# Four places for the tiles of h, and a quarter of a weight pair loaded ahead

## The chip, the cores and the metric

The kernel runs on one core of a Trainium2 chip. The metric is the device time of one execution in microseconds (us), as the median of several runs. Engines are named as in the profile: PE (TensorE, the matmuls; PEld is its weight load), DVE (VectorE), ACT (ScalarE), POOL (GpSimd) and SP (SyncE, whose queue issues almost all DMAs of this kernel). Each engine takes its own instructions in order.

## The reference

One decoder layer on x of 1024 tokens by 1024 features, in float32:

```
xn  = rmsnorm(x, attn_norm_g)
proj = xn @ w_in                      # q, k, v of two head groups, forget logits
out_a = sliding-window attention with sinks and ALiBi      # 8 heads, 2 kv heads
out_b = forgetting attention (causal, decay by cumsum of log f)   # 8 heads
h   = x + concat(out_a, out_b) @ w_out
hn  = rmsnorm(h, mlp_norm_g)
y   = h + square(relu(hn @ w_up)) @ w_down                 # w_up 1024 x 4096
```

## The kernel before

Activations are kept transposed: features on the 128 partitions, the 1024 tokens along the free axis, in two halves `left` and `right` of 512. Each float32 operand of a matmul is split into a high and a low part, and each product is three matmuls (high x high, high x low, low x high). A split is one cast, mostly on ACT, that makes the high part, and one subtraction on DVE or POOL that makes the low part (line 77 and line 80 of the helper `split`).

The order of the work is: the input projection and attention; beside the end of attention, the first half of the out projection (`out_first`: mix slices 0 to 3 of every output slice, plus x, stored to `part_d` in HBM); then the second half; then the up products; then the down products. The function that writes the kernel lists instructions in program order; a planner with a timeline of its own, under priorities, sets the order in which each engine gets them, so that an instruction can go ahead of others that precede it in the text. `tc.issue_after(ins)` keeps what is written under it behind `ins` on the same engine.

The change lies at the seam between the out projection and the up products. An output slice `dt` (0 to 7) is 128 features of h by 1024 tokens. For each, `out_products` runs 24 matmuls (mix slices 4 to 7), and `out_finish(dt, ps)` then does the following:

- it loads the first half's sum from `part_d` into a tile `h` (line 986), adds the matmul result to it on DVE (line 988, one add per token half) and stores h to `h_d` (line 989), since the end of the kernel needs h again;
- it makes the operands of the up products from it. These products use a scheme of Strassen's kind (seven products in place of eight for a 2 x 2 block), so their operands `bh[n]`, `bl[n]` are splits of h's blocks and of sums `ts` of blocks. Slices 0 to 3 and 4 to 7 are the two feature blocks. For `dt < 4` there is one split (operand 1) and one sum; for `dt >= 4` two splits (operands 2 and 3), three sums and four splits of sums (operands 6, 7, 5, 4).

Slices come in the order 0, 4, 1, 5, 2, 6, 3, 7. The products of 0 and 4 are partly done beside attention; the others follow in the loop `for dt in (1, 5, 2, 6, 3, 7)`. The tiles of h take turns in two places: slices 0 to 3 in the slot `w2`, slices 4 to 6 in `w3`; slice 7 has a place of its own, `rr`. A slot that is used again waits for the readers of its former tile, the store to `h_d` among them.

Slots are named places in SBUF (`slot(tag, ...)`), used by one tile after another. Those that matter here: `m1`, `m2`, `m3`, `r1` held mix slices 0 to 3 (read in the first half), `r0` and `m4` hold mix slices 4 and 5 (read in the second half). `r1` holds the sums `ts`. `tmp` is a small tile of 2 KB a partition, used later by the squares of h.

The up weights come in 16 pairs `j`. `up_load(j)` loads a pair with two DMAs of 512 KB into `raws[j]`; a raw pair has four quarters, `a11, a12, a21, a22`. `up_sum(j)` makes the weight sums on DVE, `up_weights(n, src)` splits one operand's weights, and `up(j)` runs the seven products in the order `UP = (1, 2, 3, 6, 7, 5, 4)`, 12 matmuls each. Pairs 0 and 1 are loaded ahead: pair 0 into `m3` behind the last mix load, pair 1 into `m2` behind the load of h's slice 5. While slices 3 and 7 are finished, the weights of product 1 for `j = 0` and for `j = 1` (quarter `a11` of pair 1) are already split; PE runs both products 1 first, back to back, and then products 2, 3, 6, 7, 5, 4 of `j = 0`. From `j = 1` on the results `hb` of the up products lie in `m2`.

Of the kernel before, what the change touches and what calls it, by code (L numbers as in the profile page):

```python
# [8 lines left out]
F32 = mybir.dt.float32  # L9
# [7 lines left out]
P = 128  # L17
D = 1024
S = 1024
KT = D // P  # L20
# [5 lines left out]
NJ = NF // 2  # L26
# [29 lines left out]
def hybrid_layer(  # L56
# [13 lines left out]
    nc = tc.nc  # L70
# [4 lines left out]
    def split(hi, lo, src, hi_eng, lo_eng):  # L75
        if hi_eng is nc.scalar:
            hi_eng.copy(hi, src)  # L77
        else:
            hi_eng.tensor_copy(hi, src)
        return lo_eng.tensor_tensor(out=lo, in0=src, in1=hi.bitcast(F32), op=ALU.subtract)  # L80
# [32 lines left out]
    def small_vectors():  # L113
# [26 lines left out]
    o = {"zl": ctx.enter_context(  # L140
        tc.tile_pool(name="zl", bufs=1, side="left", reuse_waits="tile")
    )}

    def slot(tag, name, shape, dt=F32, pool=None):
        pool = o[pool or ("zx" if tag == "w6" else "zw" if tag[0] == "w" else "zl")]
        return pool.tile([P] + shape, dt, tag=tag, name=name, bufs=1)
# [722 lines left out]
    def out_weights(dt, e0):  # L869
        i = nout[0] = nout[0] + 1  # L870
        wr = o["zw"].tile([P, 4, P], F32, tag="wor", name="wor", bufs=2)
        nc.sync.dma_start(wr, w_o[dt][:, e0 : e0 + 4, :])
        w = slot(WOS[i - 10] if i > 9 else f"w{i % 2}", "wos", [2, 4, P], F32R)
        split(w[:, 0], w[:, 1], wr, nc.scalar, nc.gpsimd)
        return w[:, 0], w[:, 1]
# [12 lines left out]
    def out_products(ps, w, es):  # L888
        wh, wl = w
        for e in es:  # L890
            j = e % 4
            for c in range(2):
                cs = slice(c * 512, (c + 1) * 512)
                mm(ps[c], wh[:, j, :], mh[e][:, cs], j == 0, False)
                mm(ps[c], wh[:, j, :], ml[e][:, cs], False, False)
            for c in range(2):
                cs = slice(c * 512, (c + 1) * 512)
                mm(ps[c], wl[:, j, :], mh[e][:, cs], False, j == 3)
# [72 lines left out]
    rr = o["zr"].tile([P, S], F32, name="rr")  # L971
    left, right = slice(0, 512), slice(512, 1024)
    part = {}

    def h_split(n, t, src, gain):
        hi, lo = bh[n][:, t, :], bl[n][:, t, :]
        part["cast"] = nc.scalar.activation(hi, src, AF.Copy, scale=gain)  # L977
        nc.vector.scalar_tensor_tensor(  # L978
            out=lo, in0=src, scalar=gain, in1=hi.bitcast(F32), op0=ALU.mult, op1=ALU.subtract
        )  # L980

    def out_finish(dt, ps):
        t, gain = dt % 4, gm[:, dt : dt + 1]
        h = slot(f"w{2 + dt // 4}", "h", [S]) if dt < 7 else rr
        with tc.issue_after(part["load"].ins) if dt == 7 else nullcontext():
            part["load"] = nc.sync.dma_start(h, part_d[dt])
        for c, cs in enumerate((left, right)):
            nc.vector.tensor_tensor(out=h[:, cs], in0=ps[c], in1=h[:, cs], op=ALU.add)
        nc.sync.dma_start(h_d[dt], h)
        if dt < 4:  # L990
            h_split(1, t, h[:, left], gain)
            ts = part["t"] = slot("r1", "ts", [4, 512])
            b12 = part["b12"] = slot("w4", "b12", [512])
            part["cast"] = nc.scalar.activation(b12, h[:, right], AF.Copy, scale=gain)
            nc.vector.scalar_tensor_tensor(
                out=ts[:, 0], in0=h[:, left], scalar=gain, in1=b12, op0=ALU.mult, op1=ALU.subtract
            )
            return
        ts, b12 = part["t"], part["b12"]
        h_split(2, t, h[:, left], gain)  # L1000
        h_split(3, t, h[:, right], gain)
        for i, q, other, op in (
            (1, right, ts[:, 0], ALU.add),
            (2, right, b12, ALU.subtract),
            (3, left, ts[:, 1], ALU.subtract),
        ):
            nc.vector.scalar_tensor_tensor(
                out=ts[:, i], in0=h[:, q], scalar=gain, in1=other, op0=ALU.mult, op1=op
            )
        part["rest"] = lambda: sum_splits(ts, t, ((0, 5), (3, 4)))  # L1010
        sum_splits(ts, t, ((1, 6), (2, 7)))
        if t < 3:
            part.pop("rest")()

    def sum_splits(ts, t, which):
        for i, n in which:
            split(bh[n][:, t], bl[n][:, t], ts[:, i], nc.scalar, nc.vector)

    raws, up_loads, up_sums = {}, {}, {}

    def up_load(j):
        raws[j] = slot({0: "m3", 1: "m2"}.get(j, f"r{j % 2}"), "wur", [2, KT, P])
        for i in range(2):
            up_loads[j] = nc.sync.dma_start(raws[j][:, i], w_u[j + i * NJ])

# [3 lines left out]
    def plus(out, a, b, eng=nc.vector):  # L1029
        eng.tensor_tensor(out=out, in0=a, in1=b, op=ALU.add)  # L1030

    def up_sum(j):
        raw = raws.pop(j)
        s = slot("m5" if j % 2 == 0 else "m4" if j > 1 else "r1", "wus", [4, 4, P])
        a11, a12, a21, a22 = raw[:, 0, :4], raw[:, 0, 4:], raw[:, 1, :4], raw[:, 1, 4:]
        plus(s[:, 0], a21, a22)
        minus(s[:, 1], s[:, 0], a11)
        minus(s[:, 2], a11, a21)
        minus(s[:, 3], a12, s[:, 1])
        return {1: a11, 2: a12, 3: s[:, 3], 4: a22, 5: s[:, 0], 6: s[:, 1], 7: s[:, 2]}  # L1040
# [3 lines left out]
    def w_slot(name, shape, dt=F32):  # L1044
        nw[0] += 1
        return slot(f"w{(1, 5, 0, 6, 3, 4, 2)[(nw[0] - 1) % NW]}", name, shape, dt)

    def up_weights(n, src):
        w = w_slot("wu", [2, 4, P], F32R)
        split(w[:, 0], w[:, 1], src, nc.scalar, nc.vector if n in (2, 6, 5) else nc.gpsimd)  # L1050
        return w
# [3 lines left out]
    for dt, ps, w in ahead_of:  # L1055
        out_finish(dt, ps)
# [7 lines left out]
    def bank(name):  # L1064
        nbank[0] += 1
        return pm.tile([P, 512], F32, tag=f"m{nbank[0] % 8}", name=name, bufs=1)

    casts = []
    for dt in (1, 5, 2, 6, 3, 7):
        w = out_weights(dt, 4)  # L1070
        ps = [bank(f"po{c}") for c in range(2)]
        out_products(ps, w, range(4, 8))
        out_finish(dt, ps)
        if dt == 5:
            with tc.issue_after(part["load"].ins):
                up_load(1)
        casts.append(part["cast"].ins)
        if dt == 3:
            up_ahead = [up_weights(1, up_sums[0][1]), up_weights(1, raws[1][:, 0, :4])]

# [3 lines left out]
    def up_products(n, w, ps):  # L1086
        for k in range(4):
            mm(ps, w[:, 0, k], bh[n][:, k], k == 0, False)
            mm(ps, w[:, 0, k], bl[n][:, k], False, False)
            mm(ps, w[:, 1, k], bh[n][:, k], False, k == 3)  # L1090
# [1 line left out]
    second = []  # L1092

    def up(j):
        if 0 < j < NJ - 1:
            up_load(j + 1)
        src = up_sums.pop(0) if j == 0 else up_sum(j)
        m = {}
        for n in UP:
            if n == 1 and j == 1:  # L1100
                m[n] = second.pop()
            else:
                with tc.issue_after(casts[-2 if n == 2 else -1]) if j == 0 else nullcontext():
                    w = up_ahead.pop(0) if n == 1 and j == 0 else up_weights(n, src[n])
                m[n] = bank(f"pu{n}")
                up_products(n, w, m[n])
            if n == 1 and j == 0:
                second.append(bank("pu1"))
                up_products(1, up_ahead.pop(), second[0])
            if n == 2 and j == 0:  # L1110
                part.pop("rest")()
            if n == 2 and j == 1:
                nbank[0] += 1
            if n == 1:
                u = slot("m1", "u", [4, 512])
                b = slot("m2" if j else "m0", "hb", [4, 512])
                nc.scalar.copy(u[:, 0], m[1])
            if n == 2:
                plus(b[:, 0], m[2], u[:, 0])
            if n == 6:  # L1120
                plus(u[:, 1], m[6], u[:, 0])
            if n == 7:
                plus(u[:, 2], m[7], u[:, 1])
            if n == 5:
                minus(u[:, 3], u[:, 1], m[5])
                minus(b[:, 2], u[:, 2], m[5])
                plus(b[:, 3], m[3], u[:, 3])
            if n == 4:
                plus(b[:, 1], m[4], u[:, 2])
        return lambda: up_end(j, b)  # L1130
# [14 lines left out]
    tmp = lambda name, n: o["zr"].tile([P, n], F32, tag="tmp", name=name, bufs=1)  # L1145
# [192 lines left out]
    for i in range(len(STEPS)):  # L1338
        down(i)
        if STEPS[i][0] == len(PHASES) - 1 and late:  # L1340
            name, dt, cs = late.pop(0)
# [65 lines left out]
```

## Time and profile before

| | us |
|---|---|
| median of 3 runs | 1085.82 |
| lowest and highest of the runs | 1085.18, 1089.3 |
| the profiled execution | 1086.83 |
| its span, first to last instruction | 1085.1 |

The span has 15578 instructions, and the mean granted TensorE clock over it is 0.998 of full speed. The stages by the trace: attention and the first half of the out projection up to 427 us, the second half up to 465 us, the up products up to 776 us, the down products to the end.

How to read it: a line of the timeline gives the start, the duration, the engine, the line of the kernel, the operation, the tile written and the tiles read, how many instructions the line merges, and in brackets how long the engine had been idle and what ended that. In a table by stretches, each row gives the stretch and its length, then busy time and instruction count of PE, PEld, DVE, ACT and (where it is not left out for want of instructions) POOL, then the granted PE clock, the busy share of the DMA engines and GB/s. A line of waits gives the total, the number of times and the longest. A line of the chain that ended last gives start, length and what held the chain. A line of DMA issues gives the count, the size of one and the median time from issue to landing.

### The profile page before, as it was taken

To read this page: it belongs to the slowest core of one execution; us is meant where nothing else is said; L and a number is where in the kernel's file an instruction comes from. 1 tells how busy PE (TensorE), PEld (TensorE's weight loads), DVE (VectorE), ACT (ScalarE), POOL (GpSimd) and SP (SyncE) were. 2 spreads that over 40 slices of the span, in tenths; PEclk is the share of its full clock that TensorE was granted. 3 is DMA by queue.
4 is the path that set the end of the run, shared out by engine and by line. 5 is a ranking of instruction groups with operands and counts; after the bars stand their busy time and mean duration, and the time that the engine had idled before them with its cause. 6 is when DMAs were issued, how large, how long until landed. Compare 5 with 4: busy or idle time off the path is not lost.

```text
span 1085.1 us, 15578 instructions
## 1 busy us (share of the span) xinstructions
PE 1072.6 (99%) x5492; PEld 932.6 (86%) x5492; DVE 780.5 (72%) x1319; ACT 574.3 (53%) x1022; POOL 384.2 (35%) x350
## 2 busy tenths in 40 slices
PE   9999999999999999999999999999999999999998
PEld 8999999999998887878888888888888888888886
DVE  7377787877775787897776869674775876764395
ACT  5558587776867765555445453534533433333331
POOL 5572423546556663213223332322222313131100
PEclk9999999999999999999999999999999999999999
DMA  8402212324746655644455443443998885665523
GB/s 289 162 14 61 61 44 65 117 90 138 245 164 251 232 191 181 228 160 171 168 186 184 175 172 136 151 158 131 354 390 311 307 296 205 229 233 190 172 85 116
DMA packets 96222, 195.67 MB, mean 180 GB/s; under 512 B 7392, under 2 KB 19856, under 8 KB 96144
## 3 DMA queue, kind: packets, MB, share of 16 engines
q1 hardware_dynamic: 95856, 194.54, 51.3%
q8 instruction: 43, 0.70, 0.3%
q14 instruction: 35, 0.29, 0.1%
q10 hardware_dynamic: 288, 0.15, 0.0%
HBM read 141.61 MB, written 53.04 MB: 179 GB/s over the span
## 4 chain that ended last, share of the span: by engine, by line
PE 90%; DVE 4%; DMA 2%; issue 1%; ACT 1%; POOL 1%; SPq 0%; ACTq 0%; DVEq 0%
PE pu L73 28%; PE pd L73 28%; PE ps L73 13%; PE po L73 7%; PE pvb L73 3%; PE spb L73 3%; PE tpb L740 3%; PE sp L73 1%; PE tpa L565 1%; PE pv L73 1%; DMA xq<-in_x_dram 1%; DMA wr<-in_w_a_dram 1%; PE ptk L331 1%; PE ptq L331 1%; DVE x L207 1%
## 5 line engine op out<-in xcount | busy, mean ns | idle before, releaser
L73 PE MATMUL pd<-hx,wx 128*128 128x512 f32 (+1 forms) x1350 | 304.9, 388 | 0.0
L73 PEld LDWEIGHTS pd<-hx,wx 128*128 128x128 f32 x1350 | 252.7, 188 | 52.2
L73 PE MATMUL pu<-bh,wu 128*128 128x512 f32 x896 | 278.0, 391 | 1.2 <-ACT bh L977 1.2
L73 PEld LDWEIGHTS pu<-bh,wu 128*128 128x128 f32 x896 | 168.9, 189 | 37.2 <-ACT bh L977 1.6
L73 PE MATMUL ps<-w,x 128*128 128x384 f32 (+1 forms) x960 | 196.5, 342 | 0.9 <-POOL w L80 0.6
L73 PE MATMUL pu<-bl,wu 128*128 128x512 f32 x448 | 175.1, 391 | 0.6 <-DVE bl L978 0.6
L73 PEld LDWEIGHTS ps<-w,x 128*128 128x128 f32 x960 | 165.1, 188 | 5.0 <-POOL w L80 1.2
L77 ACT CAST hx<-hr 128x1024 fp32r<-128x1024 f32 x56 | 59.0, 1054 | 175.5 <-PE pd L73 171.0
L80 POOL TENSOR_TENSOR wx<-wda,wx 128x1024 fp32r<-128x1024 f32 x24 | 65.3, 2720 | 195.6 <-ACT wx L77 177.3
L80 DVE TENSOR_TENSOR hx<-hr,hx 128x1024 fp32r<-128x1024 f32 x56 | 72.3, 1300 | 71.0 <-ACT hx L77 71.0
L73 PEld LDWEIGHTS pu<-bl,wu 128*128 128x128 f32 x448 | 84.5, 189 | 18.6 <-DVE bl L978 0.9
L73 PE MATMUL po<-mix,wos 128*128 128x512 f32 x384 | 93.6, 393 | 0.0
L80 POOL TENSOR_TENSOR wu<-wus,wu 128x512 fp32r<-128x512 f32 x32 | 46.4, 1451 | 129.0 <-ACT wu L77 129.0
L73 PEld LDWEIGHTS po<-mix,wos 128*128 128x128 f32 x384 | 70.7, 188 | 13.8
L80 POOL TENSOR_TENSOR wu<-wur,wu 128x512 fp32r<-128x512 f32 x32 | 43.0, 1344 | 91.5 <-ACT wu L77 91.5
L77 ACT CAST wu<-wus 128x512 fp32r<-128x512 f32 x64 | 38.4, 618 | 62.6 <-PE pu L73 56.2
L1027 DVE TENSOR_TENSOR ht<-hb 128x512 f32<-128x512 f32 x32 | 22.9, 756 | 63.2 <-ACT hb L1134 63.2
L704 ACT ACTIVATE sb<-sb,nmb 128x128 f32<-128x128 f32 (+3 forms) x64 | 49.8, 779 | 27.0 <-DVE nmb L699 26.4
L403 DVE TENSOR_TENSOR ptl<-tpb,pth 128x512 fp32r<-128x512 f32 (+1 forms) x80 | 50.0, 630 | 17.7 <-ACT pth L402 16.8
L77 ACT CAST wx<-wda 128x1024 fp32r<-128x1024 f32 x56 | 58.5, 1049 | 7.5 <-DMA wda<-in_w_d_dram 7.5
L80 POOL TENSOR_TENSOR w<-wr,w 128x384 fp32r<-128x384 f32 (+1 forms) x47 | 51.7, 1108 | 28.3 <-ACT w L77 16.8
L694 POOL TENSOR_SCALAR_AFFINE_SELECT cm<-cb 128x128 f32<-128x128 f32 (+1 forms) x64 | 31.1, 486 | 56.8 <-DVE nmb L699 56.2
(205 smaller groups left out, 1837.8 us busy)
## 6 DMA issues: line engine op xcount, KB each, us to landing
wda<-in_w_d_dram SPq DMA_DIRECT2D x34, 1024.0 KB, 9.5
hr<-hid_d SPq DMA_DIRECT2D x56, 512.0 KB, 6.3
wur<-in_w_u_dram SPq DMA_DIRECT2D x32, 512.0 KB, 4.4
hid_d<-ht SPq DMA_DIRECT2D x16, 1024.0 KB, 4.3
hid_d<-hb SPq DMA_DIRECT2D x16, 768.0 KB, 3.6
mix<-mixs_d SPq DMA_DIRECT2D x7, 1024.0 KB, 5.8
wr<-in_w_b_dram SPq DMA_DIRECT2D x32, 192.0 KB, 2.5
xq<-in_x_dram SPq DMA_DIRECT2D x8, 512.0 KB, 6.1
```

The costliest lines, as they stand in the source:

```text
L73: return nc.tensor.matmul(out, lhsT, rhs, start=start, stop=stop)
L77: hi_eng.copy(hi, src)
L80: return lo_eng.tensor_tensor(out=lo, in0=src, in1=hi.bitcast(F32), op=ALU.subtract)
L207: last_x = nc.vector.scalar_tensor_tensor(out=lo, in0=xr[:, cs], scalar=ga, in1=hi.bitcast(F32), op0=ALU.mult, op1=ALU.subtract,)
L331: nc.tensor.transpose(pt[:w, j * P : (j + 1) * P], x[:, 4 * c + j, col : col + w], ident)
L403: nc.vector.tensor_tensor(out=lo[:, cols], in0=pt[:, cols], in1=hi[:, cols].bitcast(F32), op=ALU.subtract)
L565: nc.tensor.transpose(tp[:, hh * P : (hh + 1) * P], pts[hh // 2][:, hh % 2, c0 : c0 + P], ident)
L694: nc.gpsimd.affine_select(out=cm, in_=bias, pattern=[[-1, n]], compare_op=ALU.is_ge, fill=BIG, base=n - P, channel_multiplier=1,)
L704: nc.scalar.activation(pr[:, :nk], pr[:, :nk], AF.Exp, scale=-1.0, bias=nm[:, c : c + 1], accum_out=dn_b[p % 2][:, h, i : i + 1] if p < 3 ...
L740: nc.tensor.transpose(tp[:, c0 : c0 + P], probs[qi][:, kb * P : (kb + 1) * P], ident)
L1027: eng.tensor_tensor(out=out, in0=a, in1=b, op=ALU.subtract)
```

## The change

The tiles of h get two more places. Slices 1 and 3, one after the other, lie in the first half of a new tile `h2` in slot `m2`, slice 5 in its second half; slices 0 and 2 stay in `w2`, slices 4 and 6 in `w3`, slice 7 in `rr`. The load of slice 1 is put behind the load of the up weights' pair 0, those of 5 and 7 behind the load of the slice before them.

`m2` is no longer free for the raw weights of pair 1. Only the quarter `a11` of that pair, which product 1 needs, is loaded ahead, 256 KB into the `tmp` place. The whole pair (with `a11` again) is loaded by `up(0)`, as later pairs are by the `up` before them, into `m4`, which mix slice 5 holds until the last slice's products have read it.

```diff
+    up_loads = {}
+
+    def h_tile(dt):
+        if dt == 1:
+            part["two"] = slot("m2", "h2", [2, S])
+        if dt in (1, 5, 3):
+            return part["two"][:, dt // 4]
+        return slot(f"w{2 + dt // 4}", "h", [S]) if dt < 7 else rr
+
     def out_finish(dt, ps):
         t, gain = dt % 4, gm[:, dt : dt + 1]
-        h = slot(f"w{2 + dt // 4}", "h", [S]) if dt < 7 else rr
-        with tc.issue_after(part["load"].ins) if dt == 7 else nullcontext():
+        h = h_tile(dt)
+        behind = {1: up_loads.get(0), 5: part.get("load"), 7: part.get("load")}.get(dt)
+        with tc.issue_after(behind.ins) if behind else nullcontext():
             part["load"] = nc.sync.dma_start(h, part_d[dt])
...
-    raws, up_loads, up_sums = {}, {}, {}
+    raws, up_sums = {}, {}
 
     def up_load(j):
-        raws[j] = slot({0: "m3", 1: "m2"}.get(j, f"r{j % 2}"), "wur", [2, KT, P])
+        raws[j] = slot({0: "m3", 1: "m4"}.get(j, f"r{j % 2}"), "wur", [2, KT, P])
...
         if dt == 5:
+            up_one = o["zr"].tile([P, 4, P], F32, tag="tmp", name="wu1", bufs=1)
             with tc.issue_after(part["load"].ins):
-                up_load(1)
+                nc.sync.dma_start(up_one, w_u[1][:, :4])
         casts.append(part["cast"].ins)
         if dt == 3:
-            up_ahead = [up_weights(1, up_sums[0][1]), up_weights(1, raws[1][:, 0, :4])]
+            up_ahead = [up_weights(1, up_sums[0][1]), up_weights(1, up_one)]
...
     def up(j):
-        if 0 < j < NJ - 1:
+        if j < NJ - 1:
             up_load(j + 1)
```

## The prediction

> **What bounds the kernel now.** I read the page's busy times first, then the chain that ended last, then TensorE's (PE's) waits, and then the timeline where that chain leaves PE.
>
> ```profile
> PE 1072.6 (99%) x5492; PEld 932.6 (86%) x5492; DVE 780.5 (72%) x1319; ACT 574.3 (53%) x1022; POOL 384.2 (35%) x350
> ```
>
> ```profile
> 427.25 34.10 PE po L73 x150
> 461.34 1.29 DVE h L988 x2
> 462.66 1.42 DVE ts L1007 x2
> 464.07 1.32 DVE bl L978 x2
> 467.18 1.28 DVE h L988 x2
> 469.78 190.07 PE pu L73 x830
> ```
>
> PE is busy 99% of the span, so an edit can only win where PE waits. In its second half the chain leaves PE at one place: between the out projection (po) and the up products (pu) it runs for 8 us over VectorE (DVE), which is finishing h. From 469.78 on it is PE again.
>
> ```profile
> PE pu L73 <- ACT bh L977: 1.2, 1, 1.2
> PE pu L73 <- DVE bl L978: 0.6, 1, 0.6
> ```
>
> ```profile
> 427.08 38.33 PE L73 MATMUL po<-mix,wos 128*128 128x512 f32 x168
> 465.25 0.39 PE L73 MATMUL pu<-bh,wu 128*128 128x512 f32 x1
> ...
> 468.68 0.49 PE L73 MATMUL pu<-bh,wu 128*128 128x512 f32 x1 [1.23 <-ACT bh L977]
> 469.78 0.50 PE L73 MATMUL pu<-bl,wu 128*128 128x512 f32 x1 [0.61 <-DVE bl L978]
> ```
>
> ```profile
> 465.20:474.90 9.70, 7.82 (x25) 5.79 (x26) 0.00 (x0) 0.00 (x0) 0.82 0.85 321
> ```
>
> The 168 po matmuls run from 427.08 to the first pu at 465.25: 38.17/168 = 0.2272 us each. The last fence is the table by stretches for tile pu alone; it counts 25 starts before 474.90, and the next matmul starts just after. Undisturbed, number 26 would start at 465.25 + 25 x 0.2272 = 470.93. So **4.0 us** are lost here. The tenth pu matmul (468.68) is due at 467.29 and the eleventh (469.78) at 467.52: by the eleventh 2.26 us are lost to waiting. The other 1.7 us come next:
>
> ```profile
> 471.00:474.50 3.50, 3.50 (x10) 2.71 (x9) 3.39 (x6) 2.14 (x5) 0.17 (x1) 0.51 0.64 257
> 475.00:476.00 1.00, 1.00 (x6) 0.83 (x5) 1.00 (x1) 0.98 (x3) 0.62 (x1) 1.00 0.09 33
> ```
>
> The granted clock (third number from the right) is halved from about 471 to 474.5, right behind the waits.
>
> Why h is late is read on SP's queue and DVE's timeline:
>
> ```profile
> 438.58 4.23 SPq L986 DMA_DIRECT2D h<-part_d  x2
> 442.86 0.90 SPq L1024 DMA_DIRECT2D wur<-in_w_u_dram  x2
> 445.02 0.33 SPq L989 DMA_DIRECT2D h_d<-h  x1
> 451.45 0.33 SPq L986 DMA_DIRECT2D h<-part_d  x1
> 451.87 0.38 SPq L989 DMA_DIRECT2D h_d<-h  x1
> 457.07 0.32 SPq L986 DMA_DIRECT2D h<-part_d  x1
> 457.48 0.38 SPq L989 DMA_DIRECT2D h_d<-h  x1
> 462.52 0.32 SPq L986 DMA_DIRECT2D h<-part_d  x1
> ```
>
> ```profile
> h<-part_d SPq DMA_DIRECT2D x7, 512.0 KB, 4.1
> h_d<-h SPq DMA_DIRECT2D x7, 512.0 KB, 5.1
> ```
>
> Slices finish in the order dt 0, 4, 1, 5, 2, 6, 3, 7, and each place (w2, w3) is reloaded only when the store of its last slice has landed: store of dt 2 at 457.48, load of dt 3 into the same place at 462.52, adds at 467.18. One store and one load in series, 5.1 + 4.1 us, lie between two slices of a place. PE had finished dt 3's products (24 a slice) at 427.08 + 144 x 0.2272 = 459.8, so these adds are 7.4 us behind it.
>
> **The change part by part.**
>
> *Four places.* dt 0, 2 stay in w2 and dt 4, 6 in w3; dt 1, 3 and dt 5 go to the new tile h2 in m2, whose former reader (mix slice 1) ended with the last first-half product, ahead of the 168. The loads of dt 1 and 5 move from 438.58 and about 442.5 to right behind the first up pair's load, about 423; SP pays 0.33 us for each issue either way. The load of dt 2 no longer waits for dt 1's store but for dt 0's, for which the old load of dt 1 waited until 438.58: 13 us earlier than 451.45. dt 6 follows dt 4 in w3 and is 10 or more earlier; dt 3 follows dt 1's store (445.02 + 5.1 = 450), 12 earlier; dt 7 follows dt 3. Each then lands before PE is done with its slice (dt 3: 450 + 4.1 = 454 against 459.8). Were h2 followed as one tile, dt 3 would wait for dt 5's store (451.87 + 5.1 + 4.1 = 461), still 6 us ahead of 467.18: no cost in the sum.
>
> So the load stops being the bound, and DVE is late next:
>
> ```profile
> 455.76 1.29 DVE L988 TENSOR_TENSOR h<-po,h 128x512 f32<-128x512 f32 x2 [1.95 <-DMA h<-part_d]
> ...
> 461.33 1.29 DVE L988 TENSOR_TENSOR h<-po,h 128x512 f32<-128x512 f32 x2 [0.97 <-PE po L73]
> ```
>
> ```profile
> 432.30:471.70 39.40, 37.56 (x164) 30.56 (x163) 34.66 (x54) 21.28 (x34) 8.17 (x6) 0.99 0.69 234
> ```
>
> From the first add to dt 7's adds at 471.7 DVE is busy 34.66 of 39.40 us: idle 4.74. Of this 1.95 + 0.97 = 2.92 are loads (the second names PE, but dt 6's products had ended at 427.08 + 120 x 0.2272 = 454.3; the load issued at 457.07 is what landed at 461.2). The other 1.8 are short waits on ScalarE (ACT) casts, which an earlier next slice can fill.
>
> Against this stands that two GpSimd (POOL) instructions lay in just these idle stretches:
>
> ```profile
> 434.35 3.00 POOL L80 TENSOR_TENSOR wos<-wor,wos 128x512 fp32r<-128x512 f32 x2 [3.74 <-ACT wos L77]
> ...
> 453.87 1.29 POOL L80 TENSOR_TENSOR wu<-wur,wu 128x512 fp32r<-128x512 f32 x1 [4.72 <-ACT wu L77]
> 460.23 1.29 POOL L80 TENSOR_TENSOR wu<-wur,wu 128x512 fp32r<-128x512 f32 x1 [5.07 <-ACT wu L77]
> ```
>
> ```profile
> 434.71 1.48 DVE L978 SCALAR_TENSOR_TENSOR bl<-h,vt,bh 128x512 fp32r<-128x512 f32 x1
> ...
> 474.33 2.50 DVE L978 SCALAR_TENSOR_TENSOR bl<-rr,vt,bh 128x512 fp32r<-128x512 f32 x2
> ```
>
> Beside POOL one bl takes 1.48 and two take 2.50, where two alone take 1.32: 0.8 to 1.2 us more for a collision. With the idle time gone, both (the first up weights, lows on POOL) may meet busy DVE: 2 x 0.9 = 1.8 back, from 0 to 2.4. DVE's chain then comes earlier by 4.74 - 1.8 = 2.9 us; at worst by 2.92 - 2.4 = 0.5, at best by 4.7. I take 2.9, the busy time of the measured stretch plus collisions, since DVE runs behind PE there and seldom lacks ready work. The Trainium skill (SBUF — State Buffer, "SBUF: two separate sides") says that the port pair is an exclusive lock, the loser blocked for the whole instruction; by that it is 2 x 1.29 = 2.6 back, the chain 2.1 earlier and the estimate some 0.8 later; the trace agrees that DVE is held up, for 0.8 to 1.2.
>
> How much is needed? The eleventh pu matmul needs dt 3's bl 2.26 earlier. Then PE arrives 4.0 earlier at product 2 and those behind, which need dt 7's values. Their tightest row:
>
> ```profile
> 480.83 1.88 DVE L80 TENSOR_TENSOR bl<-ts,bh 128x512 fp32r<-128x512 f32 x3
> ```
>
> The first of the three ends at about 481.5; it is read by the eleventh matmul of the fifth block of twelve (product 6), which ran at about 470.93 + 4.0 + (58 - 25) x 0.2272 = 482.4. Slack 0.9, so 3.1 are needed: 0.2 us stay. **Gain 4.0 - 0.2 = 3.8 us** (ends: 0.5 and 4.0).
>
> *A quarter of the raw weights ahead.* At dt 5 one 256 KB load replaces two of 512 KB, into the place "tmp", used by the squares from 493 on only: SP one issue fewer (0.45 us, not on the path), 0.75 MB less beside the loads of 443 to 450. The second product for j = 1 reads it as before. Cost 0; the cover is that the second block of pu starts only at 468.
>
> *The rest behind the out projection.* Both 512 KB loads go to m4, free when PE has read mix slice 5 for dt 7, 427.08 + 156 x 0.2272 = 462.5. On SP this wait stands before the second pair's load (raw 2), the last h stores and the reloads for the squares; PE waits for none of these directly. Its landing:
>
> ```profile
> 483.24 0.68 DVE L1030 TENSOR_TENSOR wus<-wur 128x512 f32<-128x512 f32 x1
> ...
> 497.21 0.69 DVE L1030 TENSOR_TENSOR wus<-wur 128x512 f32<-128x512 f32 x1 [2.40 <-DMA wur<-in_w_u_dram]
> ```
>
> ```profile
> DMA to landing us min/median/max: 3.4/7.0/8.0
> ```
>
> (The last row is that of tile wur from 420 to 500.) Issued between 462.6 and 468.5, landed by 470 to 477; its first reader on DVE stood at 483.24 and will come at about 479.4. Hidden, with 2 us in hand; without it DVE stalls in order. h2 is free long before the first hb in m2: 0.
>
> **Sum.** The profiled execution took 1086.83 us (span 1085.1 and 1.7 around): 1086.83 - 3.8 = 1083.0. The three timed runs have their median 1.0 lower, 1085.82, which gives 1082.0. I put 1082.5, between the two.
>
> **The rivals.**
> 1. *DVE becomes the bound.* The collisions cost their full 2.4 and ACT's 1.8 of waits stay, so the chain is only 0.5 to 2 earlier: PE still waits 1 to 2.6 us, with or without 1.7 of half clock. Gain 0.3 to 2.5, about 1085. For it: DVE 34.66 of 39.40 busy. Against: an in-order engine with more ready work has fewer gaps.
> 2. *The half clock is not due to the wait.* Then 1.7 stays and the gain is 2.1: 1084.2.
>
> ```profile
> 416.60:418.20 1.60, 0.58 (x4) 0.39 (x5) 1.60 (x4) 1.26 (x3) 1.60 (x1) 1.00 0.91 312
> ```
>
> Here PE was busy 0.58 of 1.60 us and the clock stayed full (third number from the right); but that pause was shorter than 2.26 and the halving followed the wait within 2 us, so I give it little. The Trainium skill (TensorE: Matmul & The Clock Gate, Part 1, "What's actually happening") has the clock halve after about 3.4 us idle; no pause here is that long, so by that rule the halving was not this wait's and the time is 1084.2; the trace, halving after 2.26 us of gaps, agrees only in part.
> 3. *Slower: the late raw load takes the wait's place.* If SP issues it behind dt 7's store (about 469) and raw 2 goes ahead of it, it lands at 469 + 2 x 8.0 = 485; DVE, due at 479.4, stands 5.6 us. 2.40 of such a wait cost PE nothing at 497.21; 3.2 would, plus 1.7 of half clock: 4.9 - 3.8 = 1.1 slower than the profiled execution, 1087.9. It decides from a landing after about 484. Against: both places are free from 462.5 and the loads are asked for in the order of j.
> 4. *The order of instructions*, which a planner sets by its own times, shifts elsewhere. The pauses of the last fence, at attention's end, are the nearest that it could close or double: about 1 to 2 us either way on the forecast, 1080.5 to 1084.5.
>
> **How the numbers follow.** Forecast (gain 3 to 4.1) 0.62, rival 1 0.15, rival 2 0.06, rival 3 0.09, rival 4 0.08. The forecast's own range is 1081.1 (1085.18, the lowest run, less 4.1) to 1083.8 (1086.83 - 3.0). Rivals 1 and 2 reach to 1086.0, rival 4 down to 1080.5: range 1080.5 to 1086.0, leaving out rival 3 and the ends of 4. 0.5% is 5.4 us, about what a measurement of this kernel can tell from no change: the forecast's gain, and all PE lost at this place, is below it. Faster by over 0.5% needs rival 4's good end, or a low draw of the forecast: 0.07. Slower by over 0.5% needs some 4 us more than rival 3 costs: 0.04. Same 0.89.
>
> **What would show it.** Right: loads of dt 1 and 5 on SP near 423, none of dt 2 to 7 waiting for the store just before it; dt 3's adds near 464; the two PE waits on bh and bl gone or under 0.3; clock 1.00 from 465 to 480; number 26 of pu at 25 x 0.2272 behind the first. Rival 1: a PE wait on bl of dt 3, or of product 2 or 6, with POOL beside DVE. Rival 2: full PE but a halved stretch. Rival 3: DVE wus waiting for wur more than 2.4. The prediction is wrong if PE waits in a place where it had none, or if the chain still leaves PE for more than 1 us at this seam.

## The result and the profile after

| | before | after |
|---|---|---|
| median of ten runs each, us | 1086.53 | 1082.84 |
| lowest and highest | 1085.18, 1089.48 | 1081.69, 1084.67 |
| the profiled execution | 1086.83 | 1082.51 |
| its span | 1085.1 | 1080.8 |

The ratio of the runs, with its 95% interval, is 0.9966 [0.9957, 0.9975]: the change gains 3.7 us of the 1087. It is the forecast's size, 3.8, but the runs below show that one of the two parts was given no share in it and could have done it alone.

The page's first part and the chain of after across the seam (asked for up to 600 us, so its last row ends there):

```profile
PE 1070.7 (99%) x5492; PEld 930.5 (86%) x5492; DVE 780.2 (72%) x1319; ACT 573.4 (53%) x1022; POOL 383.2 (35%) x350
```

```profile
426.78 38.16 PE po L73 x168
464.94 135.12 PE pu L73 x595
```

PE has its 5492 matmuls in 1.9 us less busy time (1072.6 before), and of the 4.3 us that the span lost the other 2.4 were PE idle; DVE's work is what it was. The chain no longer leaves PE at the seam: its DVE lines between po and pu are gone. Between 460 and 500 us PE's waits have no row for pu either. Three tables by stretches of after: tile pu alone at the seam, all engines over the seam, and all engines from DVE's first add of h to the last (to be held against 432.30 to 471.70 of before).

```profile
464.70:470.50 5.80, 5.72 (x26) 4.79 (x27) 0.00 (x0) 0.00 (x0) 1.00 0.83 304
```

```profile
465.00:480.00 15.00, 15.00 (x67) 12.05 (x66) 14.88 (x19) 9.74 (x18) 4.62 (x3) 1.00 0.49 178
431.80:468.20 36.40, 36.40 (x163) 30.12 (x162) 34.59 (x54) 21.29 (x34) 8.20 (x6) 1.00 0.60 213
```

The first has all 26 starts in 5.80 us, where before had lost 4.0. The second has a full PE and a clock of 1.00. The third is the same DVE work (54 instructions, 34.59 us busy against 34.66) in 36.40 us instead of 39.40: 3.0 us earlier.

For the comparisons below I measure two things in each trace. **T** is the start of the first pu matmul. The **seam loss** is how much later the 60th pu matmul starts than 59 x 0.2267 us after T (0.2267 is the distance of two pu matmuls in after where nothing holds them up). It is 4.04 in before and 0.22 in after. T itself came 0.47 earlier (465.25 to 464.78), and 0.47 + 3.82 are 4.29 of the 4.32 between the two profiled executions. T moves by more than that between executions of one kernel (465.25 and 466.10 in two traces of before), so the 0.47 isn't put down to the change.

SP's queue in after, its timeline in two stretches:

```profile
421.52 0.93 SPq L1034 DMA_DIRECT2D wur<-in_w_u_dram  x2
422.50 1.16 SPq L996 DMA_DIRECT2D h<-part_d  x2
...
438.07 4.23 SPq L996 DMA_DIRECT2D h<-part_d  x2
444.50 0.32 SPq L999 DMA_DIRECT2D h_d<-h  x1
447.16 0.32 SPq L996 DMA_DIRECT2D h<-part_d  x1
447.53 0.42 SPq L996 DMA_DIRECT2D rr<-part_d  x1
...
460.89 0.81 SPq L1034 DMA_DIRECT2D wur<-in_w_u_dram  x2
464.98 0.33 SPq L999 DMA_DIRECT2D h_d<-h  x1
465.35 1.25 SPq L1034 DMA_DIRECT2D wur<-in_w_u_dram  x2
```

Slices 1 and 5 are asked for at 422.5, 2 and 6 from 438.07, 3 at 447.16 (462.52 before) and 7 right behind it. Of the two raw pairs the first to go out, at 460.89, is pair 2: its place `r0` held mix slice 4, which PE reads last with the 150th of the 168 po matmuls, at 460.5. Pair 1 follows at 465.35, behind the store of dt 3: its place `m4` held mix slice 5, read last with the 156th, at 461.8. (e6 and e7 below, which send pair 1 behind the store of slice 7, still have the first of these loads, at 459.64 and 460.97.) The row to remember is the store at 444.50 and the load that follows it at 447.16. That load is dt 3's, into the place that this store (dt 1's) empties: 2.7 us. In before dt 1's store went out at 445.02 and the load behind it, dt 2's, at 451.45: 6.4 us. Ahead of that store in the queue stood the megabyte of raw pair 1 (442.86). I call the time from a store to the load that waits for it a turn.

### The profile page after: what moved, and what is told of

Read it like the earlier page. It is cut to its first block, busy times and chain, and to the rows that moved or that the text cites. A ratio compares the mean times of both kernels' runs of the same rounds, so it can differ in the third digit from the quotient of the medians.

```text
span 1080.8 us, 15581 instructions
## 1 busy us (share of the span) xinstructions
PE 1070.7 (99%) x5492; PEld 930.5 (86%) x5492; DVE 780.2 (72%) x1319; ACT 573.4 (53%) x1022; POOL 383.2 (35%) x350
## 4 chain that ended last, share of the span: by engine, by line
PE 72%; DVE 2%; issue 1%; DMA 0%; ACT 0%; DVEq 0%; ACTq 0%
PE pu L73 28%; PE pd L73 28%; PE po L73 8%; PE pvb L73 2%; PE ps L73 2%; PE tpb L740 2%; PE spb L73 2%; DVE ptl L403 0%; DVE sb L699 0%; DMA mix_d<-mtb 0%; PE ptk L331 0%; DVE m L1040 0%; DVE pd L1333 0%; PE ptq L331 0%; PE pms L73 0%
```

## Experiments: which part does it

Times in this and the next sections are medians; before has its own median in each group of kernels that shared a chip: 1086.86 in the first (e1 to e4), 1087.22 in the second (both kernels again, e1b, e5), 1086.85 in the third (e6 to e9).

**The second part alone** (e1, and again as e1b): h keeps its two places, and only the raw pair is moved. Against after:

```diff
 def h_tile(dt):
-    if dt == 1:
-        part["two"] = slot("m2", "h2", [2, S])
-    if dt in (1, 5, 3):
-        return part["two"][:, dt // 4]
...
-behind = {1: up_loads.get(0), 5: part.get("load"), 7: part.get("load")}.get(dt)
+behind = part.get("load") if dt == 7 else None
```

> The second part of the change alone: a quarter of pair 1 ahead, the rest behind the out projection, but h in two places as before. Theory (the gain comes from the four places, which take a store and a load in series out of DVE's way): DVE again stands for about 2.9 us in two waits on loads of h, PE waits about 2.3 us on bh and bl of slice 3 and the clock is halved for 3.4 us, time as before, 1086.5 (1085.5 to 1087). Rival (0.75 MB less traffic between 443 and 450 speeds up the stores and loads of h): the waits shrink by a microsecond or more, 1083.5 to 1085.

Measured: 1084.56, ratio 0.9982 [0.9972, 0.9993]; seam loss 0.13. So the wait is gone with two places. In the second group, beside after:

> The second part alone once more. Its first trace lost only 0.13 us at the seam but had TensorE slowed by a halved stretch at 420 to 423.6, just ahead of it, while loads went on; its runs were still 1.7 us slower than the changed kernel's. If relief of traffic does the whole work: seam loss again under 0.5 us, runs within 0.7 us of the changed kernel's. If the two places still bind and the first trace had TensorE late by luck: VectorE waits on a load of h for 0.5 to 1.5 us, seam loss 1 to 2.5, runs 1084 to 1085.5.

Measured: e1b 1083.76, 0.9972 [0.9962, 0.9981]; after 1083.89, 0.9972 [0.9961, 0.9984]. They are the same, and e1b's seam loss is 0.25 (after's second trace 0.60). In its own group e1 had gained 2.3 us, less than the change's 3.7; beside after, e1b gained 3.5 and after 3.3. SP's queue in e1b:

```profile
442.50 0.39 SPq L1083 DMA_DIRECT2D wu<-in_w_u_dram  x1
444.62 0.32 SPq L995 DMA_DIRECT2D h_d<-h  x1
447.58 0.32 SPq L992 DMA_DIRECT2D h<-part_d  x1
448.81 0.32 SPq L995 DMA_DIRECT2D h_d<-h  x1
452.98 0.32 SPq L992 DMA_DIRECT2D h<-part_d  x1
454.64 0.32 SPq L995 DMA_DIRECT2D h_d<-h  x1
457.78 0.32 SPq L992 DMA_DIRECT2D h<-part_d  x1
```

Store and load are still strictly in turn, but one turn is 3.0, 4.2 and 3.1 us instead of 6.4, 5.2 and 5.0. dt 3's load comes at 457.78, 4.7 earlier than in before, which is enough. The series of store and load that the prediction named is real, but its length was not fixed: what SP had sent just ahead of the store set it.

**The four places without the quarter** (e2): the whole raw pair goes to m4, and product 1 of `j = 1` takes its weights from there.

```diff
-            up_one = o["zr"].tile([P, 4, P], F32, tag="tmp", name="wu1", bufs=1)
             with tc.issue_after(part["load"].ins):
-                nc.sync.dma_start(up_one, w_u[1][:, :4])
+                up_load(1)
...
-    if j < NJ - 1:
+    if 0 < j < NJ - 1:
```

> The four places alone: no quarter ahead, the second product 1 takes its weights from the whole pair 1, which is loaded into m4 once slice 5 of mix is read. Theory (the quarter covers the late pair): the first raw load goes out at about 461 and lands at 466 to 468; cast 0.6, lows on POOL 1.3, so the weights are ready at 468.5 to 470.5 where PE wants them at 467.5: PE waits 1 to 3 us, 1084 to 1086.5 with a halved clock. Rival (the planner runs product 2 or something else meanwhile, or the load is early enough): no wait, 1082.8.

Measured: 1086.36, 1.0001 [0.9992, 1.001]; seam loss 2.63. The gain is gone, but PE does not stand for raw pair 1. SP's queue, ACT's timeline, and PE's:

```profile
468.36 1.25 SPq L1034 DMA_DIRECT2D wur<-in_w_u_dram  x2
```

```profile
473.15 1.64 ACT L77 CAST wu<-wus 128x512 fp32r<-128x512 f32 x3
...
477.38 0.62 ACT L77 CAST wu<-wur 128x512 fp32r<-128x512 f32 x1
```

```profile
473.80 0.50 PE L73 MATMUL pu<-bh,wu 128*128 128x512 f32 x1 [0.63 <-ACT wu L77]
...
475.72 0.50 PE L73 MATMUL pu<-bl,wu 128*128 128x512 f32 x1 [0.66 <-DVE bl L978]
```

Raw pair 1 goes out at 468.36, behind pair 2, and is first cast at 477.38. The planner has put its product 1 further back, so PE goes from product 1 of `j = 0` to product 2 at once. The first wait is for weights made of pair 0's sums (`wus`), which are no later than in after: their casts start 5.3 us behind T in both. The second is for a bl of slice 7, which PE reads with the 27th pu matmul here and with the 36th in after. The 256 KB ahead thus give PE twelve matmuls, 12 x 0.2267 = 2.7 us, that need nothing of slice 7. Without them PE loses about that much at the seam: this is what "cost 0" of the quarter rested on.

**One further place each** (e3: slice 5 alone; e4: slices 1 and 3 alone).

```diff
...
-    if dt in (1, 5, 3):
+    if dt == 5:                  # e3; e4: if dt in (1, 3):
...
```

> Three places: only slice 5 gets the new place, 1 and 3 stay in w2 with 0 and 2. Theory: from the times of the trace after, load of 2 lands at 444.5 + 5.1 + 4.1 = 453.7 where DVE comes at 453.2, load of 3 at 453.2 + 1.3 + 5.1 + 4.1 = 463.7 where DVE comes at 463.7: DVE is late by 0.5 to 1, which the 0.9 us of slack at the seam does not all hide: 1083 to 1083.8. Rival (all four places are needed, the chain through w2 binds): waits of 2 us or more, 1085 to 1086.5.

> Three places: only slices 1 and 3 get the new place, 5 stays in w3 with 4 and 6. Theory: slice 5 loads at about 442 as before, lands in time; slice 6 loads when 5's store has landed, 448.7 + 5.1 = 453.8, and lands at 458 where DVE comes at 457.8: DVE late by up to 0.5, 1082.8 to 1083.5. Rival (the chain through w3 binds as much as that through w2): slice 6 comes at 460 or later, DVE loses 2 us or more, PE waits 1.5 and the clock is halved, 1085 to 1086.5.

Measured: e3 1083.19, 0.9971 [0.996, 0.9983], seam loss 0.43, no pu wait. e4 1085.58, 0.9992 [0.9983, 1.0001], seam loss 2.02. The expectation for e4 was missed by over 2 us; its rival, that the chain through `w3` binds too, holds. SP's queue in e4:

```profile
449.37 0.32 SPq L996 DMA_DIRECT2D h<-part_d  x1
449.74 0.42 SPq L996 DMA_DIRECT2D rr<-part_d  x1
450.45 2.04 SPq L999 DMA_DIRECT2D h_d<-h  x1
456.99 0.32 SPq L996 DMA_DIRECT2D h<-part_d  x1
```

Here two loads of 512 KB (dt 3 and dt 7, early because of the extra place) stand ahead of dt 5's store, and the load of dt 6 behind that store comes 6.5 us later. PE then waits on bl:

```profile
PE pu L73 <- DVE bl L978: 1.1, 2, 0.6
```

An extra place brought the same delay back by another route: a megabyte asked for just ahead of a store that somebody waits for.

## Experiments: a megabyte ahead of the store

e1 and e4 together say that the store's delay is the cause. To try it by itself, two copies of 512 KB from the up weights to an unused tensor were put where before had loaded the raw pair, into e1 (two places, e9) and into after (four places, e8). Nothing reads them. They go from HBM to HBM, where the raw pair went to SBUF.

```diff
+            # e9: at dt 5, behind the quarter's load; e8: at dt 6, behind its load
+            for i in range(2):
+                nc.sync.dma_start(extra_d[i], w_u[1 + i * NJ]...)
```

> Two places, quarter ahead, and the same extra 1 MB at the old place. Theory (in two places the store of slice 1 stands behind this megabyte in the queue): store to next load 6 to 7.5 us in place of 3.0, VectorE waits 2 to 3 us on loads of h as in the kernel before, seam loss 3.2 without and 4.0 with a halved clock, 1086 to 1087.5. Rival (it was the quarter's own early arrival, or the place m4, that helped): no wait, 1083.5 to 1084.

> Four places, quarter ahead, and the old traffic put back: two extra copies of 512 KB (pair 1, HBM to HBM, unused) go out ahead of the store of slice 1, where the raw pair went before. This is the first part of the change with the second part's relief taken away. Theory (either part alone removes the wait: four places take the store out of the chain, the lighter queue makes the store land sooner): store of slice 1 lands some 3 us later, no add on VectorE waits, seam loss 0.2 to 0.6, 1083 to 1084. Rival (only the relief matters): VectorE waits on loads of h again, seam loss 2 to 4, 1085.5 to 1087.

Measured: e9 1088.18, 1.0018 [1.0005, 1.003]; e8 1084.92, 0.9978 [0.9965, 0.9991]. SP's queue and PE's waits in e9:

```profile
447.92 0.39 SPq L1084 DMA_DIRECT2D wu<-in_w_u_dram  x1
448.36 1.21 SPq L1086 DMA_DIRECT2D extra_d<-in_w_u_dram  x2
450.04 0.33 SPq L996 DMA_DIRECT2D h_d<-h  x1
458.59 0.32 SPq L993 DMA_DIRECT2D h<-part_d  x1
```

```profile
PE pu L73 <- ACT bh L978: 3.0, 1, 3.0
PE pu L73 <- DVE bl L979: 0.6, 1, 0.6
```

The same store is 8.5 us ahead of its load, longer than the 6 to 7.5 expected and than any turn of before, and the two waits of before are back at the same operands, the first longer by 1.8 (3.0 against 1.2). In e8 the queue reads:

```profile
444.56 1.21 SPq L1092 DMA_DIRECT2D extra_d<-in_w_u_dram  x2
446.71 0.33 SPq L1000 DMA_DIRECT2D h_d<-h  x1
453.52 0.32 SPq L997 DMA_DIRECT2D h<-part_d  x1
```

The store is as late as in before (6.8), and PE still has no wait on pu. So the two parts are two cures for one wait:

| seam loss, us | megabyte ahead of dt 1's store | not there |
|---|---|---|
| two places | 4.04 and 3.24 (before), 5.69 (e9) | 0.13 and 0.25 (e1, e1b) |
| four places | 0.36 (e8) | 0.22 and 0.60 (after) |

Four places make h indifferent to a late store; without the megabyte there is no late store. Once the loads are out of the way, the kernels that lose under 1 us there have dt 7's adds 3.3 to 3.8 us behind T (after twice, e1, e1b, e3 and e8), so the cures don't add. e8 gained 1.9 over its before, after 3.3 and 3.7 over theirs, with intervals that overlap; whether the megabyte costs anything besides the wait stays open.

One thing these runs leave out: every transfer here is on SP's queue. In before the two halves of raw pair 1 land at 447.3 and 450.2 and the store at 451.4, in the order in which SP sent them. Whether the place in this queue counts, or only the bytes in flight on the DMA engines, was not tried; it would take the same megabyte from another queue.

## Experiments: the half clock

**Both kernels again**, unchanged, gave second traces (b2 of before, a2 of after).

> The kernel before once more, for a second trace of the seam: does the halved clock always follow the wait, and what does the seam cost without it? If the wait causes the halving: halved again for 3.4 us right behind the waits, seam loss 4.0 us up to the 60th up matmul. If the halving is drawn by where a free-running window falls: in some executions none at the seam, and then the loss is not 2.3 (4.0 less 1.7) but about 3.1, since VectorE's later values are late by that much anyway. Time 1086.5 to 1087.

> The changed kernel once more, for a second trace and more runs: seam loss 0.2 to 0.4 up to the 60th up matmul; VectorE's last adds (slice 7) about 3.2 us behind the first up matmul; time 1082.5 to 1083.5. If the gain came from a lucky draw of the clock in the first trace, the loss at the seam is 1 us or more here.

Measured: b2 1087.2, 1.0001 [0.9989, 1.0012]; a2 as above. In b2 PE waits at the seam as in the first trace of before, and the clock stays full there. It is halved somewhere else. PE's timeline of b2, then its table by stretches:

```profile
469.49 0.51 PE L73 MATMUL pu<-bh,wu 128*128 128x512 f32 x1 [1.19 <-ACT bh L977]
470.59 0.50 PE L73 MATMUL pu<-bl,wu 128*128 128x512 f32 x1 [0.60 <-DVE bl L978]
...
477.04 0.50 PE L73 MATMUL pu<-bl,wu 128*128 128x512 f32 x1 [0.48 <-DVE bl L978]
```

```profile
418.00:421.50 3.50, 3.50 (x18) 3.28 (x18) 1.73 (x4) 1.29 (x3) 0.27 (x1) 0.53 0.67 224
472.00:475.50 3.50, 3.50 (x18) 2.88 (x17) 3.46 (x6) 2.29 (x5) 0.36 (x1) 1.00 0.67 273
```

The clock (third number from the right) is 1.00 behind the seam's waits and 0.53 at the end of attention. The seam loss is 3.24 with a full clock against 4.04 with the half one. dt 7's adds come 6.4 us behind T in both. So by these two traces the half clock cost 0.8 there, not 1.7: when PE isn't slowed, it meets DVE's next value too early and waits 0.48 at 477.04, a wait that the first trace didn't have.

**Keeping PE busy during the wait** (e5): twelve matmuls, later overwritten, ahead of the first matmul that waits in before.

```diff
 for k in range(4):
+    if k == 3 and idle is not None:
+        for _ in range(12):
+            mm(idle, w[:, 0, 0], bh[n][:, 0], True, True)
```

> The kernel before with 12 extra matmuls (2.7 us, results overwritten) ahead of the tenth up matmul, so that TensorE is busy through the wait, which stays. If idle time causes the half clock: clock 1.00 at the seam, loss there about 3.1 (VectorE's later values still bind), 0.9 less than before: 1085.5 to 1086. If the halving has another cause: still halved behind the seam, loss 4.0 or more, 1086.5 to 1087.5.

Measured: 1088.83, 1.0017 [1.0005, 1.0029], above both ranges. The clock is full over the seam. The seam loss is 4.85, the 2.7 us of the twelve matmuls among them, and DVE is later too: the store's turn took 7.6 us here, and dt 7's adds come 7.9 behind T in place of 6.4. PE also waits in the down stage, 2.0 us in all, where before has no wait. The larger row:

```profile
PE pd L73 <- DVE hx L80: 1.4, 3, 0.9
```

There the order of operations and tiles on PE, DVE, ACT and POOL is that of before, and this was the slowest execution of the twelve (1091.43), so why PE waits there stays open. The run settles nothing on the clock; what the half clock costs is read from b2.

## Experiments: how late may the raw pair be

After, with raw pair 1 sent behind the store of slice 7 and then loaded again behind itself, once (e6) and twice (e7), so that its first reader must wait for the last copy:

```diff
+        if j == 0:
+            with tc.issue_after(part["store"].ins):
+                up_load(1)
+                for _ in range(1):           # e7: range(2)
+                    for i in range(2):
+                        up_loads[1] = nc.sync.dma_start(raws[1][:, i], w_u[1 + i * NJ])
```

> The changed kernel with the whole raw pair 1 sent behind the store of slice 7 and read twice into the same place, so that it lands later. Theory (a late raw pair is hidden up to some 2 to 3 us on VectorE): second landing at about 482, VectorE stands 2 to 3 us, TensorE does not wait, 1083 to 1084.5. Rival (no room at all there): TensorE waits 1 us or more, 1084.5 to 1087.

> The same, read three times: landing at about 487, VectorE due at 479.7 stands 6 to 8 us. Theory (it decides from a landing after about 484): TensorE waits 2 to 5 us and the clock may be halved behind it, 1086 to 1090. Rival (the raw pair is not needed so early, weights of later products come from pair 0): no wait, 1083 to 1084.

Measured: e6 1084.05, 0.9976 [0.9964, 0.9987], seam loss 0.55. e7 1085.64, 0.999 [0.998, 0.9999]; its loss grows from 0.74 at the 60th matmul to 2.55 at the 150th. DVE's timeline and PE's waits in e7:

```profile
484.10 0.69 DVE L80 TENSOR_TENSOR wu<-wur,wu 128x512 fp32r<-128x512 f32 x1 [0.59 <-ACT wu L77]
485.87 0.69 DVE L1040 TENSOR_TENSOR wus<-wur 128x512 f32<-128x512 f32 x1 [1.08 <-DMA wur<-in_w_u_dram]
```

```profile
PE pu L73 <- POOL wu L80: 1.0, 1, 1.0
...
PE pu L73 <- ACT wu L77: 0.3, 1, 0.3
```

In e6 the second copy is sent from 473.49, lands at 480.4 and costs no such wait, on DVE either, where 2 to 3 us were expected. In e7 the last lands at 485.9, DVE waits 1.08 for it (not 6 to 8), and PE then waits for the split weights, 1.3 us in place of 2 to 5. The landing from which a late raw pair costs PE lies between the two.

## Why the prediction was right, point by point

*What bounds the kernel.* Right in place and size: of the 4.32 us between the two profiled executions 3.82 are seam loss. **Its split failed.** "The other 1.7 us" of half clock were read as a second cost on top of 2.26 of waits. b2 shows the same seam with a full clock losing 3.24: the half clock was worth 0.8.

*Why h is late.* Half right. Store and load in series was the form of it, but 5.1 + 4.1 us were taken as the price of a turn. Only a store with half a megabyte right ahead of it, or a megabyte some 2 us ahead, took that long; e1b's turns are 3.0 to 4.2. The prediction quoted the row that says so (442.86, raw pair ahead of the store at 445.02) and read past it: dt 1's turn is the longest of the three, and the whole chain is late by it.

*Four places.* Loads as forecast: slices 1 and 5 at 422.5 (said: about 423), slice 2 13.4 earlier (said: 13), slice 3 15.4 (said: 12). One of its signs did not hold: dt 3's load still waits for the store just before it (444.50, 447.16). It lands at 452.7, 11 us ahead of its adds, so that costs nothing.

*DVE late next.* The chain was to come 2.9 us earlier and came 3.0, by two errors that cancel. So its size is luck. Of the 4.74 us of idle time I had all going and 1.8 coming back in collisions with POOL. In after 36.40 - 34.59 = 1.81 idle stay, 1.6 of them waits on ACT, one of which is in DVE's timeline here; before has the same 1.6.

```profile
453.22 1.28 DVE L998 TENSOR_TENSOR h<-po,h 128x512 f32<-128x512 f32 x2
454.42 0.79 DVE L80 TENSOR_TENSOR bl<-ts,bh 128x512 fp32r<-128x512 f32 x1
...
457.22 0.69 DVE L80 TENSOR_TENSOR bl<-ts,bh 128x512 fp32r<-128x512 f32 x1 [0.69 <-ACT bh L77]
457.83 1.28 DVE L998 TENSOR_TENSOR h<-po,h 128x512 f32<-128x512 f32 x2
```

```profile
453.36 1.30 POOL L80 TENSOR_TENSOR wu<-wur,wu 128x512 fp32r<-128x512 f32 x1 [4.72 <-ACT wu L77]
457.79 1.30 POOL L80 TENSOR_TENSOR wu<-wu,wu 128x512 fp32r<-128x512 f32 x1 [3.13 <-ACT wu L77]
```

The collisions cost 0.1 (0.79 against 0.69): both POOL instructions fell beside the adds of po, two in 1.28 as ever, which read one operand from PSUM. The Trainium skill (SBUF — State Buffer, "SBUF: two separate sides") puts the lock on a DVE operation in a 2-port mode or with two SBUF inputs, and these adds have only one; the trace agrees, and the prediction, which took 2.6 from that section, had left the condition out.

*The last 0.2.* Measured 0.22 and 0.60; in the second trace PE waits 0.2 for slice 7's bl of product 2 (the 36th pu matmul), ahead of the row of product 6 from which this remainder was worked out.

*The quarter ahead, "cost 0".* The cost is right and its cover real (e2: without the twelve matmuls nearly all of the gain is lost). **The step that failed is what it left out**: the entry "0.75 MB less beside the loads" was given no gain, and e1b shows that it is worth the whole gain by itself, e9 that it is the megabyte that counts. The time came out right because the other part reaches the same floor.

*The rest behind the out projection.* Right in time, wrong in order. Pair 1 goes out at 465.35 (said: between 462.6 and 468.5), lands at 470 and 471.2 (said: by 470 to 477), and DVE reads both raw pairs without a wait:

```profile
479.71 0.68 DVE L1040 TENSOR_TENSOR wus<-wur 128x512 f32<-128x512 f32 x1
```

Said: 479.4. But SP sends pair 2 first, since mix slice 4 is read before mix slice 5, and this row, like 483.24 of before, is the first sum of pair 2; pair 1's is the one at 480.92.

*The sum.* 1082.5 said, 1082.84 measured. The prediction put the least change that can be told from none at about 0.5%; here 0.34% was told, to within 0.1% either way.

*The rivals.* 1 (DVE the bound) lost: no pu wait on bl. 2 was half right in its reason and wrong in its price: the halving isn't tied to this wait, but taking the wait away took its cost at the seam too. 3 half came true: raw 2 did go ahead of pair 1, which the prediction had argued against. But pair 1 went out behind dt 3's store and not behind dt 7's, and landed by 471.2. The point from which it was to decide, 484, was well placed: e7 with 485.9 waits, e6 with 480.4 does not. 4 did not show: what differs between the two profiled executions is the seam and T, and PE and DVE have the same order of operations and tiles in both.

## What to carry to other kernels

Where a tile's reload waits for its store, look first at what is sent just ahead of the store: a bulk load that nobody needs yet can double the turn (3.0 to 6.4 us here), and moving it may do as much as more buffers. A small load ahead can be worth its bytes by giving the engine work that needs nothing of the late value (e2). When an edit has two parts, price each as a gain and not only as a cost, and try each alone: two cures for one wait give its price once. A half-clock stretch behind a wait costs no more than the next dependence leaves PE to gain (0.8 of 1.7 us here), and whether it is there is to be read in more than one trace.

## What the runs showed of the hardware

**A store's turn depends on what was sent just ahead of it.** From a 512 KB store's issue to that of the load that waits for it: 2.7 (after) and 3.0 us (e1b) where one 512 KB load, and in e1b the quarter, went out 2 to 2.5 us before it; 4.2 (e1b) with one such load 1.2 us before it; 5.2 and 5.0 (before) right behind one; 6.5 (e4) right behind two; 6.3 to 8.5 (before twice, e5, e8, e9) where, besides such a load, 1 MB (in e9 1.25) went out in the 2 to 3 us before it.

**The clock is halved behind pauses that PE partly fills, and not every time.** At attention's end PE is busy 0.58 or 0.60 of the 1.60 us from 416.6 in before, b2 and after alike. Of 14 traces 3 have the clock halved right behind it (b2 at 418.2, e1 and e2 at 420). Of the six traces with waits of 0.4 us or more at the seam (before, b2, e2, e4, e5, e9) two have it there; the second is e9 (which has one more at 309), this row of its table by stretches:

```profile
476.00:480.00 4.00, 3.40 (x9) 2.73 (x9) 3.88 (x7) 2.01 (x5) 0.00 (x0) 0.57 1.03 423
```

The Trainium skill (TensorE: Matmul & The Clock Gate, Part 1, "What's actually happening") tells of a free-running window of 3.4 us, and of a half clock after one idle window. Leaving out the first and the last 10 us of the span, these six are the only halved stretches of the 14 traces, and each is 3.41 us long, which agrees with that length. But no pause here is as long as one (the longest is 3.0): in the 3.41 us just ahead of the halving PE was busy 1.75 to 1.79 us in four (before, b2, e1, e2), and 1.32 and 0.50 in e9. So a window in which PE is busy for half of the time was enough here; what decides in which executions it happens stays open.
